# A two-layer diffusion backbone on one core: its own tile for the modulation sums, the transposes of the MLP's start ahead of a block product, and another share-out of six tiles

## The chip, the cores and the metric

The kernel runs on one core of one Trainium2 chip. The metric is the device time of a whole execution in microseconds (us); lower is better. TensorE (PE) multiplies, VectorE (DVE) and ScalarE (ACT) work on tiles, GpSimd (POOL) does a few small operations, and SyncE (SP) issues the transfers (DMAs), all of them in the order of its program.

## The reference

Two layers work on 1024 latent tokens of width 1024, with 256 context tokens ahead of them. Each layer has a mixing part and an MLP part, and both are modulated by six vectors that come from one product with `w_mod`:

```python
mod_x = (sc_x @ w_mod[l] + b_mod[l])[:, None, :]
sh1_x, s1_x, g1_x, sh2_x, s2_x, g2_x = jnp.split(mod_x, 6, -1)
hx = rmsnorm(x, g_pre_mix[l]) * (1 + s1_x) + sh1_x
px = hx @ w_in[l]
yx, yc = hybrid_mix(px, pc, ...)     # convolution, retention, 2-D DFT, neighbourhood attention
x = x + g1_x * rmsnorm(yx @ w_out[l], g_post_mix[l])
hx = rmsnorm(x, g_pre_ffn[l]) * (1 + s2_x) + sh2_x
x = x + g2_x * rmsnorm(conv_ffn(hx, w_up[l], ffn_conv_w[l], w_down[l]), g_post_ffn[l])

def conv_ffn(h, w_up, w_conv, w_down):
    u = dwconv3(h @ w_up, w_conv)
    a, b = jnp.split(u, 2, -1)
    return (jax.nn.silu(a) * b) @ w_down
```

The context goes the same way (in the last layer only as far as it is needed). Everything is float32.

## The kernel before

A float32 matrix is split into a high and a low part of the type float32r, and a product is made of three matmuls (high by high, high by low, low by high). So each block of weights goes through three steps in `weight` (L112 to L119): SP loads 128x1024 numbers into a tile "RAW" (L114), ACT casts it into the high part "WH" (L118), DVE subtracts to get the low part "WL" (L119). There are three RAW tiles, taken in turn (`raw_tile`, L108), four WH and four WL. A load waits until the last reader of the tile that it is to fill is done. SP has one program order, so everything behind a waiting load waits as well.

The modulation vectors 2 to 6 are made by a generator, `mod_pool`. It is called for the tables 1 and 2 of three (L973), and the code of the Fourier and the retention part calls it step by step, so that its small products lie between theirs. For each of eight rows of blocks it loads 1 MB of `w_mod` into a tile "mw" (L173) and multiplies (L184). After the eighth, ACT copies the sums out of PSUM (L188) into a tile that the caller gives: before the change, the first half of a RAW tile. The copy is transposed later (L200), some vectors are formed, and the gate is stored to memory (`gate_rows`, L228), in two stores of 128 partitions by 8 single numbers. Table 1 ends in the retention part, while PE multiplies with the weights of the input projection (L333 to L335); table 2 ends later.

The MLP's up-projection is a block scheme with seven products q1 to q7 for each of 22 pairs of weight blocks, on sums and differences of the quarters of the normed input. The stretch ahead of its loop is called the transition here. It transposes the second half of the tokens (`turn_k`, L1100), modulates it on ACT (`modulate`, L1103; the quarters 0 to 3 go through two PSUM tiles "M1" into the tiles S, the quarters 4 to 7 through "M2" into a tile "HC"), makes the product q2(1), loads what the first half had left in memory (`r11`), and forms differences: `b22` and `t3` from HC, then `n1`, `t2` and `t4`, each split into high (ACT, L284) and low (DVE, L285). The first product that needs them is q7(0). n1, t2 and t4 lie in six tiles "HX".

Nothing in the program's text says when a transfer starts: the order on each engine is that of the built program, in which an instruction stands where its tiles are free.

Of the kernel before, what the change touches and what calls it, by code (L numbers as in the profile page):

```python
# [7 lines left out]
F32R = mybir.dt.float32r  # L8
# [6 lines left out]
P = 128  # L15
DEPTH = 2
N = 1024
# [11 lines left out]
def build(tc, d, out, dbg=None):  # L29
# [44 lines left out]
    def M1():  # L74
        return cur["pool"].t([P, 512], "M1", cur["tags"]["M1"])

    def M2():
        return cur["pool"].t([P, 1024], "M2", cur["tags"]["M2"])
# [29 lines left out]
    def raw_tile():  # L108
        return wp.t([P, 1024], "RAW", 3)
# [19 lines left out]
    def mod_cols(l):  # L129
        m = Mod()  # L130
        m.l = l
        m.mc = lay.t([P, 6, KT, 2], "mc")
        m.par = lay.t([P, 80], "par")
        m.a1 = lay.t([P, KT, 2], "a1")
        m.a2 = lay.t([P, KT, 2], "a2")
        m.gg = lay.t([P, 2, KT, 2], "gg")
        m.fcw = lay.t([P, 2 * FF, 3], "fcw")
        m.cw = lay.t([P, 2, 3], "cw")
        m.lgb = lay.t([P, 2, 4], "lgb")
        m.cd = lay.t([P, 4], "cd")  # L140
        sp.dma_start(out=m.par, in_=d["par"][l])
        return m
# [17 lines left out]
    def mod_pool(m, ts, w_tile, r_tile, ahead, ps=X):  # L160

        l = m.l
        work = [(t, k) for t in ts for k in range(KT)]
        ws = {}

        def load(i):
            if i < len(work):  # L170
                t, k = work[i]
                w = ws[i] = w_tile()
                sp.dma_start(out=w, in_=d["w_mod"][l, P * k : P * k + P, 2048 * t : 2048 * t + 2048])  # L173

        for i in range(ahead):
            load(i)
        pr = None
        for i, (t, k) in enumerate(work):
            load(i + ahead)
            w = ws.pop(i)  # L180
            if k == 0:
                pr = ps()
            for j in range(4):
                pe.matmul(pr[32 * j : 32 * j + 32, :], sc32[:, k, :], w[:, 512 * j : 512 * j + 512], start=(k == 0), stop=(k == KT - 1))  # L184
            yield
            if k == KT - 1:
                mr = r_tile()
                act.copy(mr, pr)  # L188
                yield
                yield  # L190
                mod_out(m, t, mr, ps)
            else:
                yield
                yield
            yield

    def mod_out(m, t, mr, ps):
        tp = ps()
        for q in range(4):
            pe.transpose(tp[:, P * q : P * q + P], mr[:, P * q : P * q + P], ident)  # L200
        tpv = tp.rearrange("p (q j s) -> p q j s", q=4, j=4)
        for jh in range(2):
            s = 2 * t + jh
            for jl in range(2):
                j = 2 * jh + jl
                dve.tensor_tensor(
                    m.mc[:, s, 4 * jl : 4 * jl + 4, :], tpv[:, :, j, 0:2],
                    m.par[:, 8 * s + 4 * jl : 8 * s + 4 * jl + 4].unsqueeze(2).to_broadcast([P, 4, 2]), ALU.add)

        if t == 0:  # L210
            dve.tensor_scalar_add(m.a1, m.mc[:, 1], 1.0)
            dve.tensor_tensor(m.a1, m.a1, gpar(m, 0), ALU.mult)
        elif t == 1:
            dve.tensor_tensor(m.gg[:, 0], m.mc[:, 2], gpar(m, 1), ALU.mult)
            gate_rows(m, 0)
        else:
            dve.tensor_scalar_add(m.a2, m.mc[:, 4], 1.0)
            dve.tensor_tensor(m.a2, m.a2, gpar(m, 2), ALU.mult)
            dve.tensor_tensor(m.gg[:, 1], m.mc[:, 5], gpar(m, 3), ALU.mult)
            gate_rows(m, 1)  # L220
# [620 lines left out]
    m = mod_cols(0)  # L841
# [36 lines left out]
    for l in range(DEPTH):  # L878
        with_ctx = l < DEPTH - 1
        m = mods[l]  # L880
# [89 lines left out]
            nf.pool.close()  # L970


        it = mod_pool(m, (1, 2), lambda: mw.t([P, 2048], "mw", 2), lambda: raw_tile()[:, 0:512], 1)  # L973

        def step(n):
            for _ in range(n):
# [4 lines left out]
        mw = Pool(f"mw{l}", bufs=1, side="right")  # L981
# [116 lines left out]
        def turn_k(n0, k, ps):  # L1098
            for i in range(4):
                pe.transpose(ps[:, P * i : P * i + P], xn[n0 + i][:, P * k : P * k + P], ident)  # L1100

        def modulate(k, ps, dst):
            act.activation(dst, ps, AF.Identity, bias=m.mc[:, 3, k, 0:1], scale=m.a2[:, k, 0:1])  # L1103

        def to_raw(n0, k, ps, dst):

            turn_k(n0, k, ps)
            modulate(k, ps, dst)
# [58 lines left out]
        def blocks(o, w, i, b, start, js=range(4)):  # L1167

            hi, lo = w
            for j in js:  # L1170
                wk = slice(512 * i + P * j, 512 * i + P * j + P)
                first, last = start and j == 0, j == 3

                pe.matmul(o, hi[:, wk], b.part(0, j), start=first, stop=False, skip_group_check=True)  # L1174
                pe.matmul(o, hi[:, wk], b.part(1, j), start=False, stop=False, skip_group_check=True)  # L1175
                pe.matmul(o, lo[:, wk], b.part(0, j), start=False, stop=last, skip_group_check=True)  # L1176
# [8 lines left out]
        def q2(f):  # L1185
            blocks(pair[f]["a"], pair[f]["a1"], 1, b21, False)
# [93 lines left out]
        hx = Pool(f"hx{l}", bufs=1, side="left")  # L1280
# [5 lines left out]
        r12 = [S() for _ in range(4)]  # L1286
        p22 = [M2() for _ in range(2)]
        for j in range(4):
            to_raw(4, j, M1(), r12[j])
            if j == 1:  # L1290
                q2(1)
        for j in range(4):
            turn_k(4, j + 4, p22[j // 2][:, 512 * (j % 2) : 512 * (j % 2) + 512])
        r22, r11 = hp_.t([P, 4, 512], "HC", 2), hp_.t([P, 4, 512], "HC", 2)
        sp.dma_start(out=r11, in_=hraw[l][0])
        b22, t3 = Half(H), Half(H)
        n1, t2, t4 = (Half(lambda: hx.t([P, 2, N], "HX", 6, F32R)) for _ in range(3))
        for j in range(4):
            modulate(j + 4, p22[j // 2][:, 512 * (j % 2) : 512 * (j % 2) + 512], r22[:, j])
        for j in range(4):  # L1300
# [310 lines left out]
```

## Time and profile before

| what | value |
|---|---|
| median of 3 runs | 2795.82 us (2795.8 to 2797.59) |
| profiled execution, its time | 2793.67 us |
| its span | 2791.9 us |
| PE busy | 2679.5 us (96%) |
| DVE busy | 1714.1 us (61%) |
| ACT busy | 1143.5 us (41%) |
| mean granted TensorE clock | 0.988 |

The span is the time from the first to the last instruction of the profiled execution, and 1.77 us lie around it. PE is idle for about 112 us in all (2791.9 less 2679.5). The granted clock is 1.00 at 2.4 GHz and 0.50 at 1.2 GHz. The median of the runs is 2.15 us above the profiled execution.

### The profile page before, as it was taken

The page shows a single profiled execution, that of the slowest core. Times are in us where ns is not written, and L with a number is a line of the kernel's source. Part 1 is how long each engine was busy: PE and PEld are TensorE (multiplying, and loading weights), DVE is VectorE, ACT ScalarE, POOL GpSimd, SP SyncE. Part 2 cuts the span into 40 slices and gives each one's busy share as a digit, 9 for nine tenths or more (in the row PEclk, how much of TensorE's full clock was granted, in tenths as well). Part 3 has the DMA queues.
Part 4 walks back from the last instruction along what each step waited for, and adds up shares of the span by engine and source line. Part 5 has one row for each costly group of instructions (what it writes and reads, how often), then busy time and mean ns, then how long its engine had stood idle before and what let it go on. Part 6 is the DMA issues. An engine that isn't in the chain of part 4 may idle for free. (4 is left out here: it accounts for less than half of the span.)

```text
span 2791.9 us, 36675 instructions
## 1 busy us (share of the span) xinstructions
PE 2679.5 (96%) x14096; PEld 2171.3 (78%) x14096; DVE 1714.1 (61%) x2917; ACT 1143.5 (41%) x1925; POOL 101.6 (4%) x142
## 2 busy tenths in 40 slices
PE   6999999998999997999999989999998999998998
PEld 4767888887788886777899867788786888887786
DVE  5444465546988887235577634555558888875434
ACT  5122344435544445224466412354445444443332
POOL 0002000010000000000000001100010000000000
PEclk9999999999999999999999999999999999999999
DMA  6641311453222225645565462222442222225534
GB/s 232 204 142 23 86 46 52 133 170 113 91 77 82 91 76 195 230 168 184 193 221 176 152 221 84 62 59 71 146 160 86 83 81 91 76 91 192 196 121 140
DMA packets 162902, 355.73 MB, mean 127 GB/s; under 512 B 49187, under 2 KB 90150, under 8 KB 156326
## 3 DMA queue, kind: packets, MB, share of 16 engines
q1 hardware_dynamic: 162726, 353.38, 38.1%
q8 instruction: 111, 1.82, 0.3%
q14 instruction: 65, 0.53, 0.1%
HBM read 292.74 MB, written 55.61 MB: 125 GB/s over the span
## 5 line engine op out<-in xcount | busy, mean ns | idle before, releaser
L119 DVE TENSOR_TENSOR WL<-RAW,WH 128x1024 fp32r<-128x1024 f32 x194 | 234.8, 1224 | 92.8 <-ACT WH L118 92.3
L118 ACT CAST WH<-RAW 128x1024 fp32r<-128x1024 f32 x194 | 200.4, 1048 | 146.4 <-PE G L310 73.3
L1402 PE MATMUL M<-WH,gh 128*128 128x512 f32 x536 | 216.1, 403 | 19.8 <-ACT gh L1443 17.5
L1444 DVE TENSOR_TENSOR gl<-gr,gh 128x384 fp32r<-128x384 f32 (+1 forms) x132 | 66.9, 511 | 253.8 <-ACT gh L1443 251.6
L1403 PE MATMUL M<-WL,gh 128*128 128x512 f32 x536 | 213.8, 399 | 0.0
L1404 PE MATMUL M<-WH,gl 128*128 128x512 f32 x536 | 212.6, 397 | 1.0 <-DVE gl L1396 1.0
L1443 ACT CAST gh<-gr 128x384 fp32r<-128x384 f32 (+1 forms) x132 | 62.6, 476 | 304.3 <-PE M L1403 284.5
L309 PE MATMUL G<-H,WH 128*128 128x512 f32 x384 | 153.1, 399 | 10.0 <-DVE nkl L695 6.0
L1174 PE MATMUL M<-H,WH 128*128 128x512 f32 x352 | 138.7, 397 | 21.3 <-ACT H L284 14.4
L1123 DVE TENSOR_TENSOR WL<-RAW,WH 128x1024 fp32r<-128x1024 f32 x88 | 107.6, 1223 | 77.3 <-ACT WH L1122 77.1
L310 PE MATMUL G<-H,WH 128*128 128x512 f32 x384 | 151.8, 395 | 0.0
L311 PE MATMUL G<-H,WL 128*128 128x512 f32 x384 | 151.5, 395 | 0.0
L1122 ACT CAST WH<-RAW 128x1024 fp32r<-128x1024 f32 x88 | 92.5, 1051 | 141.6 <-PE M L1175 79.0
L309 PE MATMUL G<-HC,WH 128*128 128x256 f32 x496 | 140.8, 284 | 0.1
L310 PE MATMUL G<-HC,WH 128*128 128x256 f32 x496 | 140.9, 284 | 0.0
L311 PE MATMUL G<-HC,WL 128*128 128x256 f32 x496 | 140.2, 283 | 0.0
L1175 PE MATMUL M<-H,WH 128*128 128x512 f32 x352 | 139.4, 396 | 0.8 <-DVE H L285 0.8
L1174 PE MATMUL G<-H,WH 128*128 128x512 f32 x352 | 138.5, 394 | 1.4 <-ACT s L1183 1.4
L1176 PE MATMUL M<-H,WL 128*128 128x512 f32 x352 | 138.6, 394 | 1.2 <-DVE WL L1123 1.2
L1174 PE MATMUL M<-HX,WH 128*128 128x512 f32 x352 | 139.6, 397 | 0.0
L1402 PEld LDWEIGHTS M<-WH,gh 128*128 128x128 f32 x536 | 101.8, 190 | 48.2 <-ACT gh L1443 19.2
L1176 PE MATMUL M<-HX,WL 128*128 128x512 f32 x352 | 138.7, 395 | 0.6 <-DVE WL L1123 0.6
(395 smaller groups left out, 6939.7 us busy)
## 6 DMA issues: line engine op xcount, KB each, us to landing
RAW<-in_w_down SPq DMA_DIRECT2D x122, 512.0 KB, 4.0
RAW<-in_w_up SPq DMA_DIRECT2D x110, 512.0 KB, 3.6
mw<-in_w_mod SPq DMA_DIRECT2D x32, 1024.0 KB, 4.8
RAW<-in_w_in SPq DMA_DIRECT2D x44, 512.0 KB, 4.1
gscr<-HC SPq DMA_DIRECT2D x44, 512.0 KB, 2.6
gr<-gscr SPq DMA_DIRECT2D x88, 192.0 KB, 3.8
R<-in_w_up SPq DMA_DIRECT2D x22, 512.0 KB, 3.6
xmid<-x SPq DMA_DIRECT2D x18, 512.0 KB, 2.6
```

The costliest lines, as they stand in the source:

```text
L118: act.copy(hi, raw)
L119: dve.tensor_sub(lo, raw, hi.bitcast(F32))
L309: pe.matmul(o, hi[:, wk], tok.cols(k, 0, c), start=(k == 0), stop=False)
L310: pe.matmul(o, hi[:, wk], tok.cols(k, 1, c), start=False, stop=False)
L311: pe.matmul(o, lo[:, wk], tok.cols(k, 0, c), start=False, stop=(k == KT - 1))
L1123: dve.tensor_sub(lo, raw, hi.bitcast(F32))
L1174: pe.matmul(o, hi[:, wk], b.part(0, j), start=first, stop=False, skip_group_check=True)
L1175: pe.matmul(o, hi[:, wk], b.part(1, j), start=False, stop=False, skip_group_check=True)
L1176: pe.matmul(o, lo[:, wk], b.part(0, j), start=False, stop=last, skip_group_check=True)
L1402: pe.matmul(o, gh[:, tsl], hi[:, ns], start=start, stop=False)
L1403: pe.matmul(o, gh[:, tsl], lo[:, ns], start=False, stop=False)
L1404: pe.matmul(o, gl[:, tsl], hi[:, ns], start=False, stop=stop)
```

## The change

Three edits. The modulation sums get a tile "ma" of their own in place of a RAW tile. In the transition, the transposes of quarter j+4 and of quarter j alternate and all of them stand ahead of q2(1), which stood after quarter 1. The six HX tiles are asked for first and then shared out in another order.

```diff
-        it = mod_pool(m, (1, 2), lambda: mw.t([P, 2048], "mw", 2), lambda: raw_tile()[:, 0:512], 1)
+        it = mod_pool(m, (1, 2), lambda: mw.t([P, 2048], "mw", 2), lambda: mw.t([P, 512], "ma", 1), 1)
...
         for j in range(4):
+            turn_k(4, j + 4, p22[j // 2][:, 512 * (j % 2) : 512 * (j % 2) + 512])
             to_raw(4, j, M1(), r12[j])
-            if j == 1:
-                q2(1)
-        for j in range(4):
-            turn_k(4, j + 4, p22[j // 2][:, 512 * (j % 2) : 512 * (j % 2) + 512])
+        q2(1)
         r22, r11 = hp_.t([P, 4, 512], "HC", 2), hp_.t([P, 4, 512], "HC", 2)
         sp.dma_start(out=r11, in_=hraw[l][0])
         b22, t3 = Half(H), Half(H)
-        n1, t2, t4 = (Half(lambda: hx.t([P, 2, N], "HX", 6, F32R)) for _ in range(3))
+
+        hxs = [hx.t([P, 2, N], "HX", 6, F32R) for _ in range(6)]
+        n1, t4, t2 = (Half(lambda i=iter(i): hxs[next(i)]) for i in ((0, 5), (1, 2), (3, 4)))
```

**Around the gate's stores.** SP's program in the first layer, retention part, before the change; "grow" is the gate in memory, "RAW" a block of weights, "mw" a block of `w_mod`:

```order
L173 DMA mw_1394<-in_w_mod 128x2048
L114 DMA RAW_1432<-in_w_in 128x1024
L228 DMA grow0_65<-gg_177 128x8x1 x2
L114 DMA RAW_1438<-in_w_in 128x1024
L173 DMA mw_1484<-in_w_mod 128x2048
L114 DMA RAW_1936<-in_w_in 128x1024
L114 DMA RAW_1942<-in_w_in 128x1024
L114 DMA RAW_1948<-in_w_in 128x1024
L173 DMA mw_1573<-in_w_mod 128x2048
L114 DMA RAW_1954<-in_w_in 128x1024
```

The same place after the change:

```order
L114 DMA RAW_1948<-in_w_in 128x1024
L173 DMA mw_1316<-in_w_mod 128x2048
L173 DMA mw_1394<-in_w_mod 128x2048
L228 DMA grow0_65<-gg_177 128x8x1 x2
L173 DMA mw_1484<-in_w_mod 128x2048
L114 DMA RAW_1954<-in_w_in 128x1024
L114 DMA RAW_2716<-in_w_in 128x1024
L173 DMA mw_1573<-in_w_mod 128x2048
L173 DMA mw_1667<-in_w_mod 128x2048
```

Five loads of weights that stood right ahead of the stores or behind them (1432, 1438, 1936, 1942 and 1948) now stand earlier; a block of `w_mod` is the first load behind the stores. Where the first three went is seen in SP's program at the start of the first layer's mixing part, first before the change (csg and tab belong to the Fourier part, cd and lgb to the second layer's retention):

```order
L114 DMA RAW_1089<-in_w_in 128x1024
L141 DMA par_9156<-in_par 128x80
L146 DMA fcw_9160<-in_fcw 128x132
L147 DMA cw_9161<-in_cw 128x6
L149 DMA lgb_9162<-in_rd 128x8
L152 DMA cd_9163<-in_rd 64x4x1 x2
L351 DMA csg_796<-in_csg 128x256
L355 DMA tab_798<-in_tdft 128x1024
```

Here only small tables stood between the two loads of the first products and csg. The same place after the change:

```order
L114 DMA RAW_1089<-in_w_in 128x1024
L114 DMA RAW_1432<-in_w_in 128x1024
L141 DMA par_9156<-in_par 128x80
L146 DMA fcw_9160<-in_fcw 128x132
L114 DMA RAW_1438<-in_w_in 128x1024
L147 DMA cw_9161<-in_cw 128x6
L114 DMA RAW_1936<-in_w_in 128x1024
L149 DMA lgb_9162<-in_rd 128x8
L152 DMA cd_9163<-in_rd 64x4x1 x2
L351 DMA csg_796<-in_csg 128x256
L355 DMA tab_798<-in_tdft 128x1024
```

Three weight loads stand among and ahead of the small tables now. The second layer shows the same pattern: its loads move ahead of its own start of the mixing part.

**The transition on ACT.** The difference of ACT's program in the first layer: "S" are the quarters 0 to 3, "HC" the quarters 4 to 7, the "WH<-R" rows are weight casts for the loop, and "H<-HC" is the high part of b22 and t3.

```order
 L1122 CAST WH<-R_6158 128x1024
-L1103 ACTIVATE S<-M_6166,mc,a_176 128x512
-L1103 ACTIVATE S<-M_6172,mc,a_176 128x512
-L1122 CAST WH<-R_6158 128x1024
+L1103 ACTIVATE S<-M_6170,mc,a_176 128x512
+L1103 ACTIVATE S<-M_6180,mc,a_176 128x512
 L1103 ACTIVATE S<-M_6190,mc,a_176 128x512
-L1103 ACTIVATE S<-M_6196,mc,a_176 128x512
+L1103 ACTIVATE S<-M_6200,mc,a_176 128x512
 L1103 ACTIVATE HC<-M_6164,mc,a_176 128x512 x2
 L1103 ACTIVATE HC<-M_6165,mc,a_176 128x512 x2
```

The second weight cast has left its place between the modulations; it now stands behind the first two "H<-HC" rows. The matching subtraction on DVE has moved as well, from ahead of the first L285 to behind the second pair of L1309, and stands ahead of the last pair of L285 that makes t2.

**The transition on SP.** The difference in the first layer; "HC<-hraw" is the load of r11, "R" and "RAW" are weights of the loop, "S<-hraw" are the loads for t4:

```order
 L1140 DMA R_6158<-in_w_up 128x1024
 L1079 DMA xmid_7_74<-x 128x1024
+L1293 DMA HC<-hraw_0_87 128x2048
 L1133 DMA RAW<-in_w_up 128x1024
 L1140 DMA R_6533<-in_w_up 128x1024
-L1295 DMA HC<-hraw_0_87 128x2048
 L1315 DMA S<-hraw_1_88 128x512 x4
```

The load of r11 has moved ahead of two weight loads; the load of R_6533 and the four loads for t4 keep their places. Their waits differ: R_6533 fills the tile of R_6158, whose last reader is the subtraction that has moved on DVE.

In the built programs the six HX tiles lie at the same bytes, role by role, before and after: n1 at 149728 and 190688, t2 at 182496 and 174304, t4 at 166112 and 157920.

## Rows read from the trace of the kernel before

**Rows 1.** The page, busy time of the engines, share of the span, instructions.

```profile
PE 2679.5 (96%) x14096; PEld 2171.3 (78%) x14096; DVE 1714.1 (61%) x2917; ACT 1143.5 (41%) x1925; POOL 101.6 (4%) x142
```

**Rows 2.** Waits of PE: line, releaser, us in total, times, longest.

```profile
PE M L1402 <- ACT gh L1443: 17.5, 2, 11.8
PE G L333 <- ACT WH L118: 16.0, 3, 8.1
PE M L1174 <- ACT H L284: 14.4, 2, 7.2
...
PE G L253 <- ACT tmp L254: 1.6, 2, 0.9
```

**Rows 3.** Timeline, PE: start, duration, line, operation, [idle before, releaser].

```profile
146.01 0.58 PE L333 MATMUL G<-WH,HC 128*128 128x256 f32 x1 [6.73 <-ACT WH L118]
...
1659.10 0.58 PE L333 MATMUL G<-WH,H 128*128 128x256 f32 x1 [8.11 <-ACT WH L118]
```

**Rows 4.** Timeline, ACT, first layer, the same place.

```profile
144.92 1.04 ACT L118 CAST WH<-RAW 128x1024 fp32r<-128x1024 f32 x1 [10.31 <-DMA RAW<-in_w_in]
```

**Rows 5.** Timeline, SP: start of the issue, its duration, line, transfer.

```profile
131.90 1.00 SPq L228 DMA_DIRECT2D grow<-gg  x2
132.96 0.59 SPq L114 DMA_DIRECT2D RAW<-in_w_in  x1
...
1644.97 1.16 SPq L114 DMA_DIRECT2D RAW<-in_w_in  x1
```

**Rows 6.** DMA issues: transfer, count, size of one, median us from issue to landing.

```profile
RAW<-in_w_in SPq DMA_DIRECT2D x44, 512.0 KB, 4.1
...
grow<-gg SPq DMA_DIRECT2D x8, 4.0 KB, 10.3
```

**Rows 7.** Windows: length, busy PE, PEld, DVE, ACT, POOL, granted clock, DMA share, GB/s.

```profile
146.00:151.30 5.30, 5.29 (x17) 3.09 (x20) 1.72 (x3) 0.17 (x1) 0.00 (x0) 0.50 0.83 340
1659.10:1663.40 4.30, 4.30 (x12) 2.41 (x13) 1.71 (x3) 1.29 (x2) 0.00 (x0) 0.50 1.00 400
669.30:677.00 7.70, 7.04 (x16) 4.98 (x17) 7.16 (x12) 4.41 (x8) 0.00 (x0) 0.50 0.10 34
```

**Rows 8.** Timeline, PE, first layer, transition.

```profile
659.06 3.07 PE L1100 MATMUL M<-c_ident,HC 128*128 128x128 f32 x24 [0.17 <-ACT S L1103]
669.34 1.22 PE L1174 MATMUL M<-H,WH 128*128 128x512 f32 x2 [7.21 <-ACT H L284]
```

**Rows 9.** Timeline, ACT, first layer, transition.

```profile
658.24 1.44 ACT L1103 ACTIVATE S<-M,mc,a 128x512 f32<-128x512 f32 x2
661.13 1.05 ACT L1122 CAST WH<-R 128x1024 fp32r<-128x1024 f32 x1 [1.46 <-DVE R L1164]
662.08 1.44 ACT L1103 ACTIVATE S<-M,mc,a 128x512 f32<-128x512 f32 x2
...
668.67 1.66 ACT L284 CAST H<-HC 128x512 fp32r<-128x512 f32 x3 [1.44 <-DVE HC L1302]
```

**Rows 10.** Timeline, DVE, first layer, transition.

```profile
669.84 0.69 DVE L1304 TENSOR_TENSOR S<-HC,S 128x512 f32<-128x512 f32 x1 [0.60 <-DMA HC<-hraw]
...
681.89 1.29 DVE L1309 TENSOR_TENSOR HC<-HC 128x512 f32<-128x512 f32 x2
...
689.68 1.29 DVE L1316 TENSOR_TENSOR S<-HC,S 128x512 f32<-128x512 f32 x2
```

**Rows 11.** Timeline, SP, first layer, transition.

```profile
663.89 0.38 SPq L1295 DMA_DIRECT2D HC<-hraw  x1
674.77 15.34 SPq L1315 DMA_DIRECT2D S<-hraw  x4
```

**Rows 12.** Timeline, DVE and SP, first layer, start of the mixing part.

```profile
62.68 1.23 DVE L119 TENSOR_TENSOR WL<-RAW,WH 128x1024 fp32r<-128x1024 f32 x1 [0.18 <-ACT WH L118]
...
67.18 0.33 SPq L351 DMA_DIRECT2D csg<-in_csg  x1
```

**Rows 13.** Timeline, PE, second layer, the first later product with a block of `w_mod`.

```profile
1672.64 1.07 PE L184 MATMUL X<-mw,sc 128*32 128x512 f32 x8
```

## The prediction

> **What bounds the kernel now.** The page comes first: PE is busy 96% of the span [rows 1], so a gain can come from two things only, its idle time (about 112 us, 2791.9 less 2679.5) and the stretches in which it works at half its clock. The list of PE's waits says where the idle time lies [rows 2]. Three of its entries have one long wait in each layer: L333 on a weight cast (16.0 us, longest 8.1), L1174 on the split of the transition (14.4, twice 7.2), and L1402, the start of the down-projection (17.5, longest 11.8). The timeline places the first: 6.73 us up to 146.01 in the first layer, 8.11 us up to 1659.10 in the second, both in the retention part [rows 3]; the missing 1.1 us of the 16.0 is a third, short one. The second lies in front of q7(0), 7.21 us up to 669.34 [rows 8], and again in the second layer. The windows behind these gaps show a granted clock of 0.50, which is 1.2 GHz [rows 7]. The question for each edit is which of these waits it touches.
>
> **The cause of the retention wait.** Followed back: PE waits for the cast at 144.92, and ACT had waited 10.31 us for the load of its weights [rows 4]. SP issued this load at 132.96, some 12 us before, directly behind the two gate stores of 131.90 [rows 5]. A weight load of this kind takes 4.1 us as a rule; the stores of 4 KB take 10.3 [rows 6]. So the load was late because it was issued late and stood behind the stores. The second layer is the same: load issued at 1644.97 [rows 5], product at 1659.10 [rows 3]. The load was issued there because one of the three RAW tiles held the modulation sums: with only two left, SP couldn't load ahead.
>
> **Edit 1, the tile "ma".** It frees the third RAW tile. In the order of the changed kernel the loads that PE waited for stand far ahead of the stores, so their casts are done long before 146 and 1659, and the first weights behind the stores are ones that are needed a good deal later. Both waits should go.
> First layer: 6.73 us of wait. Behind it PE was busy 5.29 us at clock 0.50; the same at 1.00 takes half, a saving of 2.65 [rows 7]. Together 9.4.
> Second layer: 8.11, and half of 4.30, 2.15 [rows 3, 7]. Together 10.3.
> What it costs. The early casts (1.04 us of ACT each [rows 4]) and subtractions now lie in the Fourier part and, in the second layer, one cast lies ahead of the modulated transposes L254, for which PE does wait at times (1.6 us in all, longest 0.9 [rows 2]). If every other place is covered, the cost is zero to one cast; if three casts fall on the path, 3. I take 1.5, for one cast in full and small delays of the tables that now stand behind the early loads.
>
> **Edit 2, the order of the transposes.** Before, ACT modulates two quarters (658.24, 1.44 us, so to 659.68), waits 1.46 for DVE and casts a weight block (1.05), and only then, at 662.08, modulates the next two [rows 9]. PE for its part had put q2(1) between the transposes and sent the last 24 of them together, from 659.06 [rows 8]. After the change the transposes of the third and the fourth quarter follow as soon as a tile M1 is free, q2(1) comes later, inside PE's wait, and the second weight cast stands behind the first two casts of b22 and t3, where ACT was idle 1.44 us, which covers its 1.05 [rows 9]. The fourth quarter's transpose can't start before the second is modulated (659.68) and takes about 0.5 (an estimate: 3.07/24 by four [rows 8]), so the second pair ends near 661.4 where it ended at 663.52: 2.1 earlier. Everything behind it to q7(0) is a chain on ACT and DVE with no other wait, so PE starts some 2.1 earlier than 669.34. The load of r11 (663.89 [rows 11]) now goes out ahead of two weight loads, and the 0.60 that DVE waited for it [rows 10] should go too, so DVE's chain gains up to 2.7. From 669.3 to 677.0 DVE is busy 7.16 of 7.70 us [rows 7]: PE follows DVE there. Between 2.1 and 2.7 I take 2.4, for each layer, 4.8 in all. The bounds: 1 if the moved cast doesn't fit its gap, and 3.3 if the whole hole of 2.40 between the pairs, the 0.60 and some clock come back.
> The cover for two other moved pieces: the subtraction for the second weight block (1.2 us, its kind in [rows 12]) now follows L1309 at 681.89 [rows 10], where DVE is ahead of PE; and the next R load waits for it.
>
> **Edit 3, the HX tiles.** In the built programs each role has the bytes that it had before. It is a change that does nothing: 0. In particular the 11.8 of L1402 stays [rows 2]. If it did something there, I see no reason from the rows for either sign.
>
> **The sum.** -9.4 - 10.3 - 4.8 + 1.5 = -23.0, on the profiled execution's own time of 2793.67: 2770.7. The median of the runs is 2.15 above that execution, so the prediction is 2773. I count 0.2%, 5.6 us, as the least change that this measurement can tell from none.
>
> **The rivals.**
> First, the transition's gain is taken back. The next R load fills a tile whose last reader is the moved subtraction, so SP issues it only near 682, and the four loads for t4, the first at 674.77 [rows 11], queue behind it. t4 is needed at L1316, 689.68 [rows 10], or about 687 after the gain. A load issued at 682.4 that takes even the 4.1 of a weight load [rows 6] lands at 686.5, with under 1 us to spare; it is half as large. It decides if the subtraction is done more than 1 us later than I place it. Then 4.8 goes: 2778. Chance 0.15.
> Second, a new wait behind the stores. The block of `w_mod` now is the first load behind them. In the second layer its product L184 stood at 1672.64 [rows 13] and comes 10.3 earlier, near 1662.3. The load that stood there before was used 14.1 us after its issue (1644.97 to 1659.10 [rows 3, 5]); one of 1 MB, issued in its place, lands near 1660. That is 2 us of cover; of the retention waits shown each ended at clock 0.50 [rows 7]. If one of the two retention gains goes, the time is 2783. Chance 0.13.
> Third, the clock. The idle time of 7.21 shrinks to about 5.1 and is split in two by q2(1), which now runs inside it; if the clock stays at 1.00, PE's 7.04 us of work behind it takes half, 3.5 less [rows 7]. Against that stands DVE, busy 7.16 of the same 7.70, which PE would still wait for. At the most 3.5 in each layer: 2766. Chance 0.07. The Trainium skill, "TensorE: Matmul & The Clock Gate", section Terms, counts the penalty as throttled time times (1 - K/N), half of it at half rate; by that rule alone the transitions would return 3.5 each. In the retention part, where the row shows PE without another wait, I use the same half; in the transition the row on DVE decides against it.
> Fourth, on the other side: slower. At the start of the mixing part a weight load now waits on SP for the subtraction that ends at 63.91, with the tables behind it and csg at 67.18 [rows 12]. 3.3 us are the cover. To end slower it must hold the queue some 26 us more than that cover, since 23 are gained; only a tile that is freed a stage later would do that, and the order shows none. Chance 0.03. The Trainium skill, "DMA: Bandwidth & Descriptors", section "Queues, rings and completion order", says that the transfers issued by SP use one row of rings and each ring takes its descriptors in order; by that rule these early loads delay the tables as the stores delayed the weights. The trace agrees at the stores (12 us from issue to cast).
> Fifth, the change doesn't do what it says: the loads are early but the wait moves to the WH or WL tiles, of which there are four as before. The same casts then wait for the products of the older weights. In the order they stand ahead of the Fourier part's copies, so they have room: 0.02, at 2794.
>
> **How the numbers follow.** The likeliest is the sum, 0.60, with its own range of 2767 to 2779 (the cost 0 to 3, the transitions 2 to 6.6, and a few us for the new places of the products). The rivals have 0.15 (2778), 0.13 (2783), 0.07 (2766), 0.03 (slower) and 0.02 (2794). From 2765 to 2784 leaves out the last two, and the tails of the others, 2 in 10 at most. Faster by more than 0.2% means under 2790.2: all but the last cases and a double mishap, 0.93; same 0.04; slower 0.03.
>
> **What would show it.** Right: no wait of several us on L118 at L333 near 137 or 1640, clock 1.00 there; the rows of the stores unchanged at about 10 us, with no weights waited for behind them. In the transition a second pair of L1103 right behind the first, no weight cast between them, PE's wait in front of q7(0) under 6 with q2(1) inside it, no DMA wait on L1304. The wait of 11.8 at L1402 is unchanged. Wrong: a new entry in PE's waits of more than 2 us, above all L184 on a DMA, L253 on ACT, or L1174 on HX of t4; or an R load in the transition that SP issues later than 684.

## The result and the profile after

The changed kernel takes 2772.41 us (median of 4 runs, 2769.62 to 2773.27) against 2795.81 for the kernel before (4 runs beside it): the ratio is 0.9921, 95% interval 0.9908 to 0.9933, 23.4 us less at the medians. Its profiled execution took 2772.39 us, with a span of 2770.5 (before: 2793.67 and 2791.9). The forecast was 2773. It was near for a partly wrong reason, as the experiments show: the first edit gave more than its term and the second less, and that the two cancelled is luck.

PE's waits in the changed kernel (the entries that answer to [rows 2], and those that are new):

```profile
PE M L1402 <- ACT gh L1443: 15.3, 2, 10.4
PE M L1174 <- ACT H L284: 7.8, 2, 3.9
...
PE M L1174 <- ACT WH L1122: 3.1, 2, 1.6
PE M L1100 <- ACT S L1103: 2.6, 2, 1.4
...
PE G L253 <- ACT tmp L254: 1.6, 2, 0.9
...
PE G L333 <- ACT WH L118: 1.1, 1, 1.1
```

The wait on L118 has fallen from 16.0 to 1.1: both retention waits are gone and only the third, short one is left. L284 has fallen from 14.4 to 7.8. L1100 has 2.6, the waits among the transposes. The entry of L1122 (3.1, twice 1.55) was not forecast; it was 0.7 each before. So two entries are new or grown to more than 2 us in total, which the prediction had named as a sign of being wrong.

SP around the gate's stores and at the start of the first layer's mixing part, in time order (timeline of the changed kernel):

```profile
52.77 1.56 SPq L114 DMA_DIRECT2D RAW<-in_w_in  x3
...
60.86 0.33 SPq L114 DMA_DIRECT2D RAW<-in_w_in  x1
...
64.08 0.33 SPq L114 DMA_DIRECT2D RAW<-in_w_in  x1
...
66.28 0.55 SPq L351 DMA_DIRECT2D csg<-in_csg  x1
...
132.40 1.01 SPq L228 DMA_DIRECT2D grow<-gg  x2
135.33 0.34 SPq L173 DMA_DIRECT2D mw<-in_w_mod  x1
139.26 1.79 SPq L114 DMA_DIRECT2D RAW<-in_w_in  x2
```

The weights that PE waited for before are issued from 54 to 64 instead of at 132.96. The load that waits for the subtraction goes out at 64.08, and csg at 66.28, even a little earlier than before [rows 12]. The stores are where they were and land in 10.7 us (median of 8; 10.3 before). The window of the changed kernel over the place where PE stood still (columns as in [rows 7]):

```profile
130.00:150.00 20.00, 19.52 (x157) 15.97 (x156) 5.99 (x19) 4.26 (x10) 0.00 (x0) 1.00 0.74 163
```

PE is busy 19.52 of 20 us and the clock stays at 1.00. The missing 0.48 is one wait for the block of `w_mod` behind the stores. Now the transition, first layer, from the timelines of the changed kernel (PE, then ACT, DVE and SP):

```profile
650.40 1.53 PE L1100 MATMUL M<-c_ident,HC 128*128 128x128 f32 x12 [1.25 <-ACT S L1103]
658.56 0.83 PE L1174 MATMUL M<-H,WH 128*128 128x512 f32 x2 [3.88 <-ACT H L284]
...
649.57 3.17 ACT L1103 ACTIVATE S<-M,mc,a 128x512 f32<-128x512 f32 x4
656.32 1.07 ACT L1122 CAST WH<-R 128x1024 fp32r<-128x1024 f32 x1
...
658.37 0.69 DVE L1304 TENSOR_TENSOR S<-HC,S 128x512 f32<-128x512 f32 x1
...
651.74 0.33 SPq L1293 DMA_DIRECT2D HC<-hraw  x1
...
672.92 0.33 SPq L1140 DMA_DIRECT2D R<-in_w_up  x1
673.34 4.52 SPq L1315 DMA_DIRECT2D S<-hraw  x4
```

This answers to [rows 8] to [rows 11]. Four modulations stand in a row, the cast is behind the first high parts, the wait ahead of q7(0) is 3.88, with q2(1) (651.68 to 654.68) done ahead of it, and L1304 no longer waits for r11. The load of R goes out some 21 us after r11's, as the rival had it.

### The profile page after: what moved, and what is told of

It is laid out like the page before. It is cut to its first block, busy times and chain, and to the rows that moved or that the text cites. A ratio compares the mean times of both kernels' runs of the same rounds, so it can differ in the third digit from the quotient of the medians.

```text
span 2770.5 us, 36682 instructions
## 1 busy us (share of the span) xinstructions
PE 2677.6 (97%) x14096; PEld 2172.9 (78%) x14096; DVE 1712.1 (62%) x2917; ACT 1142.7 (41%) x1925; POOL 101.3 (4%) x142
## 5 line engine op out<-in xcount | busy, mean ns | idle before, releaser
L118 ACT CAST WH<-RAW 128x1024 fp32r<-128x1024 f32 x194 | 200.4, 1048 | 138.0 <-PE G L310 79.7
L1402 PE MATMUL M<-WH,gh 128*128 128x512 f32 x536 | 216.8, 404 | 17.7 <-ACT gh L1443 15.3
L1123 DVE TENSOR_TENSOR WL<-RAW,WH 128x1024 fp32r<-128x1024 f32 x88 | 107.6, 1223 | 77.5 <-ACT WH L1122 77.5
L1122 ACT CAST WH<-RAW 128x1024 fp32r<-128x1024 f32 x88 | 92.5, 1051 | 142.5 <-PE M L1175 78.6
L1174 PE MATMUL G<-H,WH 128*128 128x512 f32 x352 | 138.6, 394 | 1.4 <-ACT s L1183 1.4
L1402 PEld LDWEIGHTS M<-WH,gh 128*128 128x128 f32 x536 | 102.2, 191 | 46.2 <-ACT gh L1443 17.0
```

Of the source, the lines that this page charges most:

```text
L118: act.copy(hi, raw)
L1123: dve.tensor_sub(lo, raw, hi.bitcast(F32))
L1402: pe.matmul(o, gh[:, tsl], hi[:, ns], start=start, stop=False)
```

## The experiments

Executions of one kernel differ by a few us (the runs of the kernel before lie between 2793.6 and 2802.3 in the whole study), so the stages are read apart. Two stretches of PE's timeline serve for it in every run: from the first L333 of a layer to its first L574 (the retention stage, edit 1), and from the first transposes of the transition to q7(0), to the first product of pair 2 (the one that waits for L1122), to that of pair 3 and to the end of the last product of the up-projection (edit 2).

**Each edit alone.** The three edits are those of the diff, one at a time on the kernel before; the fourth kernel is the changed one with the old line for n1, t2 and t4.

> The kernel before with the first edit alone (the modulation sums in a tile of their own). Theory of the sum: both retention waits (6.73 and 8.11) and the half clock behind them go, less the cost of the earlier casts: 17 to 20 us faster, near 2777; the transition keeps its 7.21 twice. Rival, the edits need each other (the freed tile also helps the transition): under 12 us faster.

> The kernel before with the second edit alone (all transposes ahead of q2(1)). Theory of the sum: 2 to 5 us faster, near 2792; the wait ahead of q7(0) falls from 7.2 to about 3.9 and 1.3 appears among the transposes; the retention waits keep 6.7 and 8.1. Rival, the late weights of the next pair take it back: no change within 1 us.

> The kernel before with the third edit alone (the six HX tiles shared out in another order). Theory: the built order of every engine and the bytes of each role are as before, so 0 us; what differs is what the measurement leaves open. Rival, tile names or places matter: over 3 us in either direction.

> The changed kernel without its third edit. Theory: as the changed kernel, 23 us faster than before, with the same waits; its profile shows also which of the stretches at half clock (near 1075, 1400 and 2120 in the changed kernel) come back in another execution of the same order. Rival, the third edit has an effect: over 3 us from the changed kernel.

| kernel | median us (runs) | ratio to before, 95% interval |
|---|---|---|
| tile "ma" alone | 2774.65 (4) | 0.9924 (0.9908 to 0.9939) |
| transposes alone | 2796.05 (11) | 0.9993 (0.9984 to 1.0001) |
| HX alone | 2798.22 (11) | 1.0007 (0.9998 to 1.0016) |
| changed, old HX | 2774.19 (4) | 0.9919 (0.9905 to 0.9932) |
| before, beside them | 2796.12 (21) | 1 |

The first edit carries nearly all of it: 21.5 us, over the 17 to 20 expected. The second comes to 2 us (0.07%; the interval reaches from 4.5 us faster to 0.3 slower), under its forecast and not told from none. The third is nothing: with line numbers and tile names left out, the built order of each engine and its waits are the same with and without it, so the 2 us in its row show what two medians of one order can differ by.

The retention stage, in us:

| | first layer | second layer |
|---|---|---|
| before, HX alone, transposes alone | 117.1, 117.8, 117.5 | 149.1, 148.8, 149.3 |
| changed (four kernels) and "ma" alone (twice) | 107.6 to 108.1 | 137.1 to 137.7 |
| four more with "ma" (W3H on GpSimd, q2(1) after the third quarter, the two with the gap filled) | 107.6 | 137.3, 138.8, 138.6, 138.6 |
| before, stores on ACT | 114.6 | 147.1 |

(The four are the changed kernel, its second run, the one with the old HX and the one with its stores on ACT; the kernels of the last two rows come further down.) Over the ten with "ma" that is 9.9 less in the first layer and 11.5 in the second, from median to median of the first row. In three of the ten a wait of 1.4 to 1.6 us at L540 on DVE, which the other seven don't have, makes the second layer longer; why is not shown. The time from the start to the first L333 grew by 0.5 in the mean (81.9 to 82.3 with a RAW tile for the sums, 82.1 to 83.0 with "ma").

**Late, or behind the stores?** The kernel before and the changed one with the stores on ACT's queue:

```diff
-            sp.dma_start(out=grow[m.l][which, s].rearrange("(k p) -> p k", p=P), in_=m.gg[:, which, :, s])
+            act.dma_start(out=grow[m.l][which, s].rearrange("(k p) -> p k", p=P), in_=m.gg[:, which, :, s])
```

> The kernel before, with the gate's small stores issued by ACT instead of SP; the modulation sums stay in a RAW tile, so the load that PE waited for is still issued late. Theory that standing behind the stores is what costs: the load lands in about 4 us, the retention waits of 6.7 and 8.1 fall to under 1, 15 to 20 us faster. Rival, the late issue alone costs (the load could not be issued before 132.9): the waits keep over 4 us each, under 10 us faster. Rival, the rings are shared: no change.

> The changed kernel with the gate's small stores issued by ACT. Theory: no load that PE waits for stands behind them any more (0.5 us at most), so 0 to 1 us faster than the changed kernel. Rival, ACT's own issue of the stores holds its casts: 1 to 3 us slower.

On the kernel before this gave 2790.28 (10 runs), ratio 0.9975 (0.9966 to 0.9984): 7 us faster, a third of what "ma" gives. On the changed kernel it gave 2776.21 (4 runs), 0.9927 (0.9912 to 0.9943): no gain. In the first of the two, SP, ACT, PE and the transfers read so (timelines, then DMA issues in the stretch from 127 to 148 us):

```profile
131.37 0.33 SPq L114 DMA_DIRECT2D RAW<-in_w_in  x1
...
132.30 1.39 ACTq L228 DMA_DIRECT2D grow<-gg  x2
...
143.88 1.04 ACT L118 CAST WH<-RAW 128x1024 fp32r<-128x1024 f32 x1 [5.71 <-DMA RAW<-in_w_in]
...
145.25 0.66 PE L540 MATMUL M<-rw,rot 128*64 128x128 f32 x8 [3.02 <-ACT rot L508]
...
1658.37 0.36 PE L333 MATMUL G<-WH,H 128*128 128x256 f32 x1 [3.95 <-DVE rv L496]
...
RAW<-in_w_in SPq DMA_DIRECT2D x6, 512.0 KB, 7.5
grow<-gg ACTq DMA_DIRECT2D x2, 4.0 KB, 13.9
```

The one load directly behind the stores in the kernel before (issues from 132.5 to 134 us), and the windows in which the loads lie beside the stores, first the kernel before, then with the stores on ACT (columns as in [rows 7]; the last number is GB/s):

```profile
RAW<-in_w_in SPq DMA_DIRECT2D x1, 512.0 KB, 11.9
...
133.00:143.20 10.20, 6.28 (x51) 5.10 (x49) 2.58 (x5) 1.04 (x1) 0.00 (x0) 1.00 0.70 27
143.30:144.90 1.60, 0.00 (x0) 0.00 (x0) 0.00 (x0) 0.00 (x0) 0.00 (x0) 0.87 0.95 358
```

```profile
129.00:137.00 8.00, 8.00 (x68) 7.03 (x66) 2.42 (x12) 1.05 (x1) 0.00 (x0) 1.00 0.93 318
137.10:143.80 6.70, 5.13 (x36) 4.01 (x34) 2.64 (x3) 1.05 (x1) 0.00 (x0) 1.00 1.28 69
```

With the stores on ACT a cast still waits 5.71 us for its load, and ACT and DVE pass the delay on to PE by other tiles (3.02 and, later, 2.21 in the first layer; 3.95 and 1.99 in the second). The load of this cast was issued at 131.37, 0.9 us ahead of the stores and on another queue; it was in use at 143.88, over 12 us later. Up to 137.10 other loads ran ahead of it, and then all transfers together moved 69 GB/s. On one queue they had moved 27 until the stores were done, and 358 after that. So the theory that a load off the stores' queue lands in about 4 us has failed: the stores slow the loads on either queue. The median of 7.5 hides this, since it holds two loads that landed in 7.4 and 7.6 us before the slow stretch. What did change is the time of issue: SP no longer stands until the gate's numbers are ready, and the second load, which PE waited for before, goes out at 129.69 in place of 132.96 and lands at 137.10. A free RAW tile gives more (21.5 us), since with it the loads are issued long ahead of the stores. How much of the waits came from the late issue and how much from the stores is not told apart by these kernels. The Trainium skill, "DMA: Bandwidth & Descriptors", section "Queues, rings and completion order", says that a DMA engine takes turns between the queue rows that it has work for; the trace agrees in so far as loads on one queue and stores on another slow each other (the stores take 13.9 us instead of 10.3), but no run here shows the turns themselves.

**Where the second edit's gain goes.** Two kernels take away what was suspected, in the changed kernel: the one puts the cast W3H of pair 3 on GpSimd, the other moves q2(1) ahead of the last transposes.

```diff
+            if f == 3:
+                hi, lo = fu.t([P, 512], "W3H", 2, F32R), fu.t([P, 512], "W3L", 2, F32R)
+                pool.tensor_copy(hi, raw)
+                dve.tensor_sub(lo, raw, hi.bitcast(F32))
+                w["a22"] = hi, lo
+                return
```

```diff
             to_raw(4, j, M1(), r12[j])
-        q2(1)
+            if j == 2:
+                q2(1)
```

> The changed kernel, with the one weight cast (W3H of the pair 3) that stands ahead of ACT's table load done on GpSimd instead. Theory: this cast holds the table load by 0.6 to 0.8 us, so PE's wait at the first product of pair 2 falls from 1.55 to 0.7 in both layers and no half clock follows it: 2 to 5 us faster than the changed kernel. Rival, the wait comes from the late load: it stays 1.5, no change.

> The changed kernel with q2(1) after the third quarter's transposes instead of after the fourth's. The weight cast then stands ahead of the fourth modulation, the cast W3H goes back behind the table load, and the next R load no longer waits. Theory: q7(0) starts about 1 us later than in the changed kernel and the 1.55 becomes 0.7: within 2 us of the changed kernel, rather faster. Rival, the start of q7(0) is all that counts: 2 us slower than it.

The first gave 2771.09 (4 runs), 0.9907 (0.9894 to 0.9921); the second 2776.22 (5 runs), 0.9926 (0.9914 to 0.9939). Why a cast should matter is seen in the timelines. In the kernel before, ACT and then PE ahead of pair 2:

```profile
703.78 1.28 ACT L1230 ACT_TABLE_LOAD   x1 [1.78 <-DVE HC L344]
...
706.51 1.05 ACT L1122 CAST WH<-RAW 128x1024 fp32r<-128x1024 f32 x1
...
707.61 0.50 PE L1174 MATMUL M<-H,WH 128*128 128x512 f32 x1 [0.72 <-ACT WH L1122]
```

In the changed kernel:

```profile
691.77 0.62 ACT L1122 CAST W3H<-R 128x512 fp32r<-128x512 f32 x1 [1.97 <-PE M L1175]
692.41 1.28 ACT L1230 ACT_TABLE_LOAD   x1
...
695.13 1.05 ACT L1122 CAST WH<-RAW 128x1024 fp32r<-128x1024 f32 x1
...
696.23 0.50 PE L1174 MATMUL M<-H,WH 128*128 128x512 f32 x1 [1.55 <-ACT WH L1122]
```

With the cast on GpSimd (its lines stand six further down):

```profile
692.00 2.19 POOL L1151 CAST W3H<-R 128x512 fp32r<-128x512 f32 x1 [46.67 <-PE M L1181]
...
692.00 1.28 ACT L1236 ACT_TABLE_LOAD   x1 [2.00 <-DVE HC L344]
...
695.83 0.50 PE L1180 MATMUL M<-H,WH 128*128 128x512 f32 x1 [0.95 <-ACT WH L1122]
```

The order that the transposes brought about has put one W3H cast ahead of ACT's table load. It waits for PE until 691.77, so the table load, the activation and the weight cast behind it come later, and PE waits 1.55 instead of 0.72. Off ACT, it is 0.95, so the cast is a cause of the longer wait. With q2(1) after the third quarter the wait is 0.72 again, but q7(0) then starts 14.6 and 14.9 after the first transposes, no earlier than before the change: the fourth modulation now waits for the weight cast. That is further than the 1 us expected, and the time (0.9926) is not told from the changed kernel's.

**The clock, and both again.** Ten extra matmuls ahead of q7(0), whose sums q7(0) overwrites:

```diff
                 w["cd"] = M2()
+                if f == 0:
+                    for i in range(10):
+                        pe.matmul(w["cd"][:, 512:1024], w["s31"][0][:, 0:P], b11.part(0, i % 4), start=True, stop=True, skip_group_check=True)
```

> The changed kernel as it is, beside the next three on the same chip. Theory: 0.992 of before; it gives the time against which the first edit alone, the filled gap and the moved cast are read.

> The first edit alone, a second time. Theory that the second edit's gain at the start of the loop is mostly taken back behind it: 0 to 2 us slower than the changed kernel. Rival, the second edit is worth its 2.4 for each layer: 4 to 5 us slower than the changed kernel.

> The changed kernel with ten more matmuls ahead of q7(0) in each layer, on operands that lie ready; what they write is overwritten by q7(0). They fill PE's wait of 3.9 us there. Theory that DVE sets the pace behind it: the granted clock stays at 1.00, and the time falls by under 1 us for each layer. Rival, the half clock costs its half: 2 to 3 us for each layer, 4 to 6 us faster than the changed kernel. Third, the extra matmuls hold the real ones: slower.

> The changed kernel with both: the one W3H cast on GpSimd and the ten extra matmuls ahead of q7(0). Theory: the two gains add, 2 to 5 us faster than the changed kernel, near 2770. Rival, what the cast gave was chance: no better than the filled gap alone.

| kernel | median us (runs) | ratio to before, 95% interval |
|---|---|---|
| the changed kernel | 2773.47 (4) | 0.9917 (0.9903 to 0.9930) |
| tile "ma" alone | 2774.48 (5) | 0.9918 (0.9905 to 0.9932) |
| changed, gap filled | 2774.17 (4) | 0.9919 (0.9905 to 0.9932) |
| changed, gap filled and W3H on GpSimd | 2773.76 (4) | 0.9919 (0.9906 to 0.9933) |
| before, beside them | 2796.20 (9) | 1 |

All four are alike. The windows from q7(0) on, in the changed kernel (both layers):

```profile
658.50:666.00 7.50, 6.78 (x21) 4.70 (x22) 7.50 (x13) 4.54 (x9) 0.00 (x0) 0.77 0.00 0
2080.70:2088.00 7.30, 7.30 (x21) 5.16 (x22) 7.30 (x13) 4.49 (x8) 0.00 (x0) 0.65 0.00 1
```

and with the gap filled (both layers):

```profile
657.60:665.00 7.40, 5.90 (x21) 3.61 (x22) 7.40 (x13) 4.49 (x8) 0.00 (x0) 1.00 0.00 0
2080.00:2087.50 7.50, 7.06 (x21) 5.06 (x22) 7.50 (x13) 4.45 (x8) 0.00 (x0) 0.77 0.01 3
```

The ten matmuls shorten the wait of 3.9 to 1.6 and hold the clock in the first layer only; in the second it still falls. At full clock PE does the same 21 matmuls in 5.90 instead of 6.78 to 7.30, but DVE is busy for the whole window in each of them, and the products of pair 2 start no earlier (49.6 after the first transposes, against 49.4 and 49.5). The kernel with both shows the same within one program: the clock falls there in its first layer (0.77) and stays in its second, and pair 2 starts at 48.9 in either. What W3H on GpSimd had given, 2771.09, did not come back beside the filled gap, so it can't be told from chance; no version here is shown to beat the changed kernel.

The transition's intervals, mean over layers, in us from the first transposes; the last two rows split the new order by the clock between pair 2 and pair 3:

| order | layers | q7(0) | pair 2 | pair 3 | end of the up-projection |
|---|---|---|---|---|---|
| old (before, HX alone, "ma" twice, stores on ACT) | 10 | 14.0 | 51.5 | 65.7 | 438.6 |
| new (transposes alone, changed twice, old HX, changed with stores on ACT, gap filled) | 12 | 11.9 | 49.7 | 63.9 | 437.5 |
| new, clock stays at 1.00 | 5 | 11.9 | 49.6 | 63.0 | 436.2 |
| new, clock falls to 0.50 for a while | 7 | 11.9 | 49.7 | 64.6 | 438.4 |

## Why the prediction was right

**Edit 1.** The mechanism was right as it stands: the wait was that of a load issued late, behind stores that kept it from moving, and the free tile took both waits and the half clock with them.

The term for the first layer was 9.4 and the stage lost 9.9. The term for the second was 10.3 and the stage lost 11.5. What the second term hadn't counted are a wait of 0.28 on the load of csg, which went too, and about 1 us of the products L184 with `w_mod`. The cast ahead of L254 that the cost term had in mind did cost 0.70 there, but took the place of a wait of 0.70 for a block of `w_mod`. By the view of lines over the retention stage, first the kernel before, then "ma" alone:

```profile
L184 PE MATMUL X<-mw,sc 128*32 128x512 f32 x120 | 21.0, 611 | 0.7 <-DMA mw<-in_w_mod 0.7
```

```profile
L184 PE MATMUL X<-mw,sc 128*32 128x512 f32 x120 | 19.1, 604 | 0.7 <-ACT tmp L254 0.7
```

The same 120 matmuls cost 1.9 us less. The difference lies in one block of eight, which stood in two parts around the retention wait; PE's timeline, the kernel before and then "ma" alone:

```profile
1659.61 1.92 PE L184 MATMUL X<-mw,sc 128*32 128x512 f32 x2
...
1663.81 1.06 PE L184 MATMUL X<-mw,sc 128*32 128x512 f32 x6
```

```profile
1642.93 1.07 PE L184 MATMUL X<-mw,sc 128*32 128x512 f32 x8
```

Half of the 1.92 is the half clock, which the term of 2.15 has already; the other 0.95 or so is the price of the two parts. With 8.11, 2.15 and 0.28 that makes the 11.5. The cost at the start was about 0.5. So the two terms less the cost came to 18.2, and the edit gave 21.5 and 21.7 in two measurements; their intervals reach down to 17 and 19, so it is the stages, 21.4 in all, that show the term as too small.

The rule of the Trainium skill on the clock ("TensorE: Matmul & The Clock Gate", section Terms: half of the throttled time is lost at half rate) agrees with the retention stage of the first layer, where half of 5.29 is 2.65 and PE's busy time fell by 2.77 (110.47 to 107.70 with "ma" alone).

**Edit 2.** The step to q7(0) was right to 0.1: 2.1 us earlier in the mean of the layers. What failed is the step behind it, "between 2.1 and 2.7 I take 2.4", which put what follows q7(0) at no price. By pair 3 the gain is 1.7 in the mean: 3.5 for both layers where the sum had 4.8, and the whole time shows only 1 (against "ma" alone measured beside it) to 2 us (alone), neither clear of none. I had followed the first weight cast, the subtraction and the R load, and not the W3H cast, which is seen in the order; it makes the wait of 1.55 ahead of pair 2. That wait by itself costs nothing by pair 3: where the clock stays, pair 3 starts 2.6 earlier than in the old order, and the gain is still 2.3 at the end of the up-projection. The price is the clock. Behind this wait it fell to 0.50 for a while in 7 of the 12 layers with the new order, and in none of the 10 with the old one, where the wait is 0.72; in these 7 the gain is 1.1 by pair 3 and 0.2 at the end of the up-projection. Two windows of the changed kernel, each from pair 2 to pair 3, one without and one with it, and a part of the second:

```profile
696.00:710.00 14.00, 12.48 (x52) 9.46 (x52) 14.00 (x17) 7.81 (x10) 0.00 (x0) 1.00 0.33 114
2118.00:2133.00 15.00, 13.60 (x50) 10.36 (x50) 15.00 (x17) 7.86 (x10) 0.00 (x0) 0.89 0.37 125
2120.00:2123.00 3.00, 3.00 (x8) 2.31 (x8) 3.00 (x6) 1.72 (x2) 0.00 (x0) 0.50 0.24 94
```

That the fall makes the difference is read from layers that came out so by themselves; no kernel holds the clock there on purpose. With W3H on GpSimd, where the wait is 0.95, it fell in 1 of 4 layers.

**Edit 3** does nothing, as said.

**The rivals.** The first (the gain taken back by the late R load) came near in its price (3 to 4 of the 4.8 are missing in the whole time) and had the wrong path. The load did go out late, and DVE waited for the loads of t4, for which PE did not wait:

```profile
677.90 0.69 DVE L1316 TENSOR_TENSOR S<-HC,S 128x512 f32<-128x512 f32 x1 [0.38 <-DMA S<-hraw]
679.42 0.69 DVE L1316 TENSOR_TENSOR S<-HC,S 128x512 f32<-128x512 f32 x1 [0.83 <-DMA S<-hraw]
```

The second (a wait behind the stores) came to 0.48 in the first layer and nothing in the second. The third (the clock in the transition) is decided by the filled gap where it held the clock: full clock, no gain. The fourth was not seen: csg went out at 66.28. (Its 26 us are the whole hold; beyond its cover of 3.3 it would be 23.) The fifth was not seen either: L333 waits 1.1 in all for L118.

So the two errors, 3.3 too little for the first edit and some 3 too much for the second, cancelled in the sum. That the total came out within 1 us is luck. The 11.8 of L1402 is still there at 10.4.

What stays open: what decides in which layers the clock falls behind a wait of 1.55. The mean gain of 1.1 for each layer at the end of the up-projection fits the 1 to 2 us of the totals, whose intervals are wider than that.

## What to carry to other kernels

A load that waits for a tile is late twice, by the wait and by what SP issues in the meantime; when PE waits for a weight, look at who holds the tile and what went out just ahead on the queue. After a reorder, read the order of every engine up to the next point where PE waits, not only the instructions that the edit names: a 0.6 us cast that slipped ahead of a table load made a wait of 1.55 us, and where the clock fell behind it most of the gain was gone. And test the edits one at a time even when the total fits, since terms with errors of opposite sign make a good sum.

## What was not expected of the hardware

Waits of under 2 us did leave the clock at 0.50 behind them in some layers and not in others of the same program (1.55 us: 7 of 12). The wait of 2.6 to 3.2 at the end of the MLP left it at 1.00 in both layers of the profiled execution of the kernel before, but it fell behind this wait in 24 of the 28 layers of all profiled executions; in the changed kernel a row shows 2.80 there, with the clock at 0.66 in the window from 1075 to 1080:

```profile
1075.40 0.75 PE L1174 MATMUL M<-H,WH 128*128 128x512 f32 x1 [2.80 <-DVE S L1214]
```

Two products with `w_mod` in a row take as long as eight (1.04 and 1.07 us at full clock). Each lasts 0.6 us, but in a row of eight four of them start within 0.02 us.

While two stores of 4 KB each (single numbers of 4 bytes) were under way, all transfers together moved 27 GB/s with the loads on the same queue and 69 with the loads on another, against 318 to 358 just before or after.
